# The second half of a v step: one piece per expert pair, or one piece per column half

## The chip, the cores and the metric

One Trainium2 chip, one core of it. The metric is the device time of one execution in microseconds, lower is better. The kernel before takes 3645.47 us, the median of three runs (3643.04 to 3650.47).

## What is computed

One encoder layer over 512 tokens of width 2048: two attention branches, gates, an output product, a layer norm, then PEER, a retrieval over 16384 experts, and a last layer norm. The change lies in PEER. Cut to it, the reference is:

```python
q = (h @ wq).reshape(bsz, s, PEER_HEADS, 2, PEER_HALF)
sc = jnp.einsum('bshpc,hpnc->bshpn', q, keys)
...                        # top 16 of each half, then top 16 of the sums: experts, and g by a softmax
def block(args):
    xt, et, gt = args
    a = jnp.einsum('td,thkd->thk', xt, u_tab[et])
    w = gt * jax.nn.gelu(a, approximate=False)
    return jnp.einsum('thk,thkd->td', w, v_tab[et])
```

Each token takes 128 expert rows of `u_tab` and of `v_tab`, 2048 wide, in float32.

## The kernel before

**Dense and gathered.** For 352 tokens the kernel does not gather: it goes through all 16384 experts with products on TensorE (u: scores of every expert; v: weighted sum), and the weight matrix is zero where an expert was not chosen. For the other 160 tokens it gathers rows of 1 MB (128 x 2048 float32) by an indirect DMA (L1083) and adds them up on VectorE (L1058 for u rows, L1064 for v rows). Both kinds of work run at the same time in the last 1500 us.

**Pieces.** Every matrix that TensorE needs comes as a stream of pieces of 128 x 1024 float32, 512 KB, in one fixed order (`seq`). Class `Stream` loads a piece on SP's queue (L80, tile `raw`), splits it into a high part `whi` on ScalarE (L99) and a residual `wlo` on VectorE (L100), since a product in float32 is made of three in a rounded form: high by high, high by low, low by high. `get` hands out the next piece and first calls `fill`, which sends out the splits of up to three pieces ahead and the loads of up to six. There are five buffers each for `raw`, `whi` and `wlo`. So the place of a `get` in the program sets where the split of a later piece stands in the queues of ScalarE and VectorE.

**Order.** `pin` keeps an instruction in program order on its engine. In the stage looked at here nearly all work of ScalarE, VectorE, POOL and TensorE is pinned.

**A round.** 128 experts make a chunk, four chunks (GE = 4) a group. For each group the kernel makes 4 u steps and, for the group before it, 4 v steps, one after the other: u step, v step, u step, v step. A u step (`u_mm`) takes two pieces, 24 products on each, and its Gelu (L1235) gives the scores of one chunk. Then `weigh` multiplies them with the gates (L1143 on VectorE) and splits the result into `W_h` (L1146, ScalarE) and `W_l` (L1147, VectorE). A v step (`v_mm`, index j) makes 512 columns of the output for all four chunks: four units of 128 columns (dd), each 12 products, 3 for each chunk x (L1181 to L1183). It takes two pieces, 24 products each in all. After each unit ScalarE evicts the bank (L1185) and puts the running sum of a later unit back into a bank (L1163), and an entry of `beside` is called: L1143 after unit 0, L1146 and L1147 after unit 1. After the last group of u, four v steps and then a stage of v steps alone follow, for 14 groups whose scores were made earlier and wait in memory; the last of these groups has its own form of the product (`v_part`).

**Gathered rows.** After each u step and each v step, `step` calls `gather` once or twice, by a rate of about 1.5. One call lets POOL copy one column of the youngest residual into the row's buffer (`paced`, L296), which holds the row back until that split is done, starts the row's DMA (L1083), and then lets VectorE use the row that was started two calls earlier. There are three row buffers.

**The v pieces before.** Piece x of step j of a group holds 512 columns for two chunks: chunk 0 and 1 in piece 0, chunk 2 and 3 in piece 1. Both are taken by `get` at the head of the step (L1169), and every unit uses both.

Of the kernel before, what the change touches and what calls it, by code (L numbers as in the profile page):

```python
# [19 lines left out]
P = 128  # L20
# [10 lines left out]
GE = 4  # L31
NG = 128 // GE
# [10 lines left out]
NF = sum(UQ) + UG * NCH  # L43
# [83 lines left out]
def tile_encoder_layer(ctx: ExitStack, tc: tile.TileContext, a: dict, out: bass.AP):  # L127
# [75 lines left out]
    def piece(k):  # L203
        if k[0] == "u":
            return a["u_t"][k[1], k[2]]
        if k[0] == "v":
            return a["v_t"][k[1], k[2], k[3]]
        return a["wst"][where[k]]
# [3 lines left out]
    def pin(op, level=1):  # L212


        if inorder[0] >= level:
            tc.keep_in_program_order(op)
        return op

    st = Stream(nc, wp, [(k, piece(k)) for k in seq], pin, 0, 0)
# [107 lines left out]
    with pool("p0", 3, "right") as p0:  # L327
# [70 lines left out]
        for i in range(8):  # L398
            g, t = i // 4, i % 4
# [14 lines left out]
        for g in range(2):  # L414
            vh, vl = [vp.tile([P, 4, 512], F32R, tag="v", name=f"va{g}{n}", bufs=4) for n in "hl"]
# [244 lines left out]
    with pool("attB", 2, "right") as wk:  # L660
# [7 lines left out]
        def v_b(grp):  # L668
            pss = [bank("sc") for _ in range(3)] + [bank("tp")]
            for k2 in range(2):  # L670
                wh, wl = st.get("vb", grp, k2)
                for kk in range(2):
                    k = k2 * 2 + kk
                    s = slice(kk * 512, kk * 512 + 512)
                    lh, ll = latn[4 + k]
                    for t in range(NT):
                        ts_ = slice(t * P, (t + 1) * P)
                        mm3(pss[t], (lh[:, ts_], ll[:, ts_]), (wh[:, s], wl[:, s]), k == 0, k == 3)
            return [split_to(wk, pss[t], f"v{t}", bufs=1) for t in range(NT)]

        prev = None
        v = None
        qr = {}
        for h in range(H + 1):
# [20 lines left out]
            if h < H and h % 4 == 0:  # L705
                v = v_b(h // 4)
# [449 lines left out]
    def o_bank():  # L1156
        nu[0] += 1
        return ob_[(nu[0] - 1) % 6]

    def copy_in(u):  # L1160

        if 16 <= u < nunits:
            pin(nc.scalar.activation(ob_[u % 6][:, :TD], accT[:, u % 16], AF.Copy), 2)  # L1163

    def v_mm(g, j, by=None, beside=()):

        v = [st.get("v", g, j, x) for x in range(2)]  # L1169
        beside = list(beside)  # L1170
        for dd in range(4):
            u = nu[0]
            o = o_bank()[:, :TD]
            sum_ = accT[:, j * 4 + dd]
            for x in range(GE):
                vh, vl = v[x // 2]
                wh, wl = W[g, x]
                s = slice(x % 2 * 512 + dd * P, x % 2 * 512 + (dd + 1) * P)
                first, last_ = u < 16 and x == 0, x == GE - 1
                kw = dict(skip_group_check=u >= 16)  # L1180
                pin(nc.tensor.matmul(o, vh[:, s], wh, start=first, stop=False, **kw), 2)  # L1181
                pin(nc.tensor.matmul(o, vh[:, s], wl, start=False, stop=False, **kw), 2)  # L1182
                pin(nc.tensor.matmul(o, vl[:, s], wh, start=False, stop=last_, **kw), 2)  # L1183
            if by is None:
                pin(nc.scalar.activation(sum_, o, AF.Copy), 2)  # L1185
            else:
                pin(nc.scalar.activation(sum_, o, AF.Copy, scale=by[:, j * 4 + dd : j * 4 + dd + 1]), 2)
            copy_in(u + 4)
            f = beside.pop(0) if beside else None
            if f is not None:  # L1190
                f()
        for f in beside:
            f()
# [27 lines left out]
    with pool("peer", 2, "right") as wk:  # L1221
# [8 lines left out]
        for n, g in enumerate(gorder):  # L1230
            gt = load_g(wk, g)
            for j in range(GE):
                gl = gl_of(g, j)
                ps = u_mm(g * GE + j)
                pin(nc.scalar.activation(gl, ps[:, :TD], AF.Gelu), 2)  # L1235
                if n > 0 or j > 1:
                    step()
                work = weigh(gl, gt, g, j)
                if n > 0:
                    v_mm(gorder[n - 1], j, None, work)  # L1240
                    step()
                else:
                    for f in work:
                        f()
# [11 lines left out]
    with pool("fin", 1, "right") as wk:  # L1256
# [36 lines left out]
        last = NF // GE - 1  # L1293
# [71 lines left out]
        for g in range(last + 1):  # L1365
# [19 lines left out]
            for j in range(GE):  # L1385
# [4 lines left out]
                elif j < 2:  # L1390
                    os_ = [start_sum(t, j) for t in range(ND)]
                    v = [st.get("v", g, j, x) for x in range(2)]
# [26 lines left out]
def _lay(inp):  # L1419

    f = lambda n: np.asarray(inp[n])
    w_in = f("w_in")[0]
    b_in = f("b_in")[0]
    o_q, o_k, o_v, o_c, o_kr, o_g = 0, 1024, 2048, 3072, 4096, 4160

    def fold(w):
        return w.reshape(-1, P, P).transpose(1, 0, 2).reshape(P, -1)

    def pairs(w, i):
        return w.reshape(-1, 2, P, 512)[i].transpose(1, 0, 2).reshape(P, 1024)  # L1430

    kr = w_in[:, o_kr : o_kr + 64]
    kr = np.concatenate([kr, kr], 1)
    uq = f("w_uq")[0].reshape(512, H, 192)
    ukv = f("w_ukv")[0].reshape(512, H, 256)
    pa, pb, wo, wq = f("w_pa")[0], f("w_pb")[0], f("w_o")[0], f("peer_wq")[0]

    def gcol(i):
        return o_g + (i % 2) * D + (i // 2) * P

    def piece(n, *k):
        hs = lambda w: fold(w[k[1] * 1024 : (k[1] + 1) * 1024])
        if n == "lat":
            return w_in[k[0] * P : (k[0] + 1) * P, o_c : o_c + 1024]
        if n == "va":
            return w_in[k[0] * P : (k[0] + 1) * P, o_v : o_v + 1024]
        if n == "kr":
            return fold(kr[k[0] * 1024 : (k[0] + 1) * 1024])
        if n in ("qa", "ka"):
            c = (o_q if n == "qa" else o_k) + k[0] * P  # L1450
            return hs(w_in[:, c : c + P])
        if n == "g":
            c = gcol(k[0])
            return hs(w_in[:, c : c + P])
        if n == "uqr":
            h = 4 * k[0]
            return fold(np.concatenate([uq[:, h + 2 * j : h + 2 * j + 2, 128:].reshape(512, P) for j in range(2)], 0))
        if n == "qk":
            return fold(np.concatenate([uq[:, k[0], :128], ukv[:, k[0], :128]], 0))
        if n == "vb":  # L1460
            return pairs(ukv[:, 4 * k[0] : 4 * k[0] + 4, 128:].reshape(512, 512), k[1])
        if n in ("pa", "pb"):
            return fold((pa if n == "pa" else pb)[:, k[0] * P : (k[0] + 1) * P])
        if n == "wo":
            return wo[k[0] * P : (k[0] + 1) * P, k[1] * 1024 : (k[1] + 1) * 1024]
        return hs(wq[:, k[0] * P : (k[0] + 1) * P])

    bt = [b_in[o_c + i * P : o_c + (i + 1) * P] for i in range(8)]
    bt.append(np.concatenate([b_in[o_kr : o_kr + 64]] * 2))
    bt += [b_in[i * P : (i + 1) * P] for i in range(16)]  # L1470
    bt += [b_in[gcol(i) : gcol(i) + P] for i in range(2 * KT)]
    x = f("x")[0]
    rel = np.clip(np.arange(P)[:, None] - np.arange(S)[None, :] + 384, -63, 256) + 63
    u = f("peer_u")[0]
    v = f("peer_v")[0]
    freq = (np.float32(10000.0) ** (-np.arange(0, 64, 2, dtype=np.float32) / np.float32(64.0))).astype(np.float32)
    rot = np.zeros((P, 2), np.float32)
    rot[:, 0] = np.tile(freq, 4)
    rot[:, 1] = np.tile(np.repeat(np.array([-1.0, 1.0], np.float32), 32), 2)
    return {  # L1480
        "x": x,
        "x_t": x.T.reshape(KT, P, S),
        "c_t": f("c").reshape(KT, P).T,
        "positions": f("positions").reshape(1, S),
        "w_ada_t": f("w_ada")[0].T.reshape(96, P, D),
        "b_ada_t": f("b_ada")[0].reshape(96, P).T,
        "wst": np.stack([piece(*k) for k in weight_keys()]),
        "b_in_t": np.stack(bt, 1),
        "b_va": b_in[o_v : o_v + 1024].reshape(1, 1024),
        "rms_g": np.concatenate([f("q_norm_g")[0].reshape(4, P), f("kv_norm_g")[0].reshape(4, P)]).T,  # L1490
        "rel_t": f("rel_bias")[0][:, rel],
        "rot_c": rot,
        "iota": np.tile(np.arange(P, dtype=np.float32), (P, 1)),
        "ln1_t": np.concatenate([f("ln1_g")[0].reshape(KT, P), f("ln1_b")[0].reshape(KT, P)]).T,
        "ln1_g": f("ln1_g"), "ln1_b": f("ln1_b"), "ln2_g": f("ln2_g"), "ln2_b": f("ln2_b"),
        "keys_t": f("peer_keys")[0].reshape(16, P, P).transpose(2, 0, 1).reshape(P, 16 * P),
        "u_t": u.reshape(P, P, 2, 8, P).transpose(1, 2, 4, 3, 0).reshape(P, 2, P, 1024),
        "v_t": v.reshape(P, NG, 2, 2, 4, 512).transpose(1, 4, 2, 0, 3, 5).reshape(NG, 4, 2, P, 1024),
        "peer_u": u,
        "peer_v": v,  # L1500
    }
# [17 lines left out]
```

## Time and profile before

| | us |
|---|---|
| median of 3 runs | 3645.47 |
| lowest, highest | 3643.04, 3650.47 |
| the profiled execution: its time | 3657.82 |
| its span, first to last instruction | 3656.0 |
| TensorE busy in it | 3568.4 (98%) |
| VectorE busy | 2695.8 (74%) |
| ScalarE busy | 1727.1 (47%) |
| GpSimd busy | 1002.2 (27%) |

A profile shows one execution. Times count from the first instruction. Engines: PE is TensorE's products, PEld its weight loads, DVE is VectorE, ACT ScalarE, POOL GpSimd, SP the queue that loads the pieces. In a row of the order in time, the first number is the start, the second how long it took; a bracket at the end gives how long the engine had been idle and what ended that; "x2" are two instructions of a kind in a row, merged. An engine's idle time counts only where TensorE, or the end, waits for it.

### The profile page before, as it was taken

Reading aid. Unit: us, or ns where it says so; the run is one execution under the profiler, and the core shown is the slowest. Engines: PE = TensorE matmul, PEld = TensorE weight load, DVE = VectorE, ACT = ScalarE, POOL = GpSimd, SP = SyncE. Lnnn points to the kernel's source line nnn. Section 1 sums busy time; section 2 is a strip of 40 time slices with the busy share of each in tenths; the row PEclk is TensorE's granted clock in tenths of the full one; section 3 lists DMA queues with packets and bytes.
Section 4 is the critical chain, followed back from the end, with each engine's and each line's share of the span. In section 5 each row is a group of like instructions: output and inputs, shape, how many; then the busy total and the mean of one; then the engine's idle time right before and its main releaser. Section 6 shows DMA issues by size and latency. Waiting matters only on the chain. (4 is left out here: it accounts for less than half of the span.)

```text
span 3656.0 us, 52881 instructions
## 1 busy us (share of the span) xinstructions
PE 3568.4 (98%) x20127; PEld 3285.5 (90%) x20127; DVE 2695.8 (74%) x3754; ACT 1727.1 (47%) x3072; POOL 1002.2 (27%) x1068
## 2 busy tenths in 40 slices
PE   8999999999999999999999999999999999899998
PEld 6888888887787889999999999999999999899997
DVE  8756587545555779988888678888777788677776
ACT  3233332233333455435666345555544455566763
POOL 0001110011120000002322344444454544455531
PEclk9999999999999999999999999999999999999999
DMA  9646488744356655446998899999989999799982
GB/s 395 259 164 227 165 303 301 261 141 130 115 193 241 203 197 159 130 132 234 339 349 329 313 355 357 351 365 360 355 327 343 331 362 368 298 345 341 346 326 93
DMA packets 216207, 996.71 MB, mean 273 GB/s; under 512 B 26817, under 2 KB 34161, under 8 KB 159345
## 3 DMA queue, kind: packets, MB, share of 16 engines
q1 hardware_dynamic: 131904, 525.93, 40.4%
q0 software_dynamic: 73104, 431.48, 31.5%
q10 hardware_dynamic: 10944, 35.94, 2.5%
q8 instruction: 157, 2.57, 0.3%
q14 instruction: 98, 0.79, 0.1%
HBM read 930.42 MB, written 61.51 MB: 271 GB/s over the span
## 5 line engine op out<-in xcount | busy, mean ns | idle before, releaser
L99 ACT ACTIVATE whi<-raw 128x1024 fp32r<-128x1024 f32 x800 | 822.7, 1055 | 773.8 <-PE main L160 491.9
L100 DVE TENSOR_TENSOR wlo<-raw,whi 128x1024 fp32r<-128x1024 f32 x800 | 959.4, 1221 | 284.1 <-ACT whi L99 280.0
L159 PE MATMUL q<-dh,whi 128*128 128x352 f32 x1680 | 546.2, 325 | 0.6 <-ACT glf L926 0.6
L161 PE MATMUL q<-dh,wlo 128*128 128x352 f32 x1680 | 542.1, 323 | 0.7 <-DVE wlo L100 0.7
L160 PE MATMUL q<-dl,whi 128*128 128x352 f32 x1680 | 542.5, 323 | 0.0
L296 POOL COPY row<-wlo 128x1 f32<-128x1 f32 x320 | 326.4, 1020 | 714.5 <-DVE wlo L100 519.7
L1064 DVE SCALAR_TENSOR_TENSOR h2g<-row,au,h2g 128x2048 f32<-128x2048 f32 x127 | 298.4, 2349 | 101.9 <-DMA row<-in_peer_v,gidx 99.3
L159 PE MATMUL main<-hh,whi 128*128 128x512 f32 x912 | 352.9, 394 | 10.1 <-ACT hh L354 9.9
L160 PE MATMUL main<-hl,whi 128*128 128x512 f32 x912 | 357.1, 392 | 0.0
L161 PE MATMUL main<-hh,wlo 128*128 128x512 f32 x912 | 349.4, 393 | 0.0
L1058 DVE SCALAR_TENSOR_TENSOR row<-row,h2g 128x2048 f32<-128x2048 f32 x128 | 292.6, 2288 | 76.8 <-DMA row<-in_peer_u,gidx 76.4
L161 PEld LDWEIGHTS q<-dh,wlo 128*128 128x128 f32 x1680 | 316.6, 188 | 1.0 <-DVE wlo L100 1.0
L159 PEld LDWEIGHTS q<-dh,whi 128*128 128x128 f32 x1680 | 316.5, 188 | 1.0 <-ACT glf L926 0.8
L160 PEld LDWEIGHTS q<-dl,whi 128*128 128x128 f32 x1680 | 317.0, 189 | 0.0
L1185 ACT ACTIVATE accT<-o 128x352 f32<-128x352 f32 x480 | 219.5, 458 | 184.2 <-PE o L1183 178.6
L300 DVE SCALAR_TENSOR_TENSOR adaw<-adaw,cond 128x2048 f32<-128x2048 f32 x96 | 218.8, 2291 | 100.7 <-DMA adaw<-in_w_ada_t 96.9
L159 PE MATMUL main<-qh,whi 128*128 128x352 f32 (+2 forms) x752 | 242.9, 323 | 7.5 <-ACT qs L950 7.4
L161 PE MATMUL main<-qh,wlo 128*128 128x352 f32 (+2 forms) x752 | 242.7, 323 | 0.0
L160 PE MATMUL main<-ql,whi 128*128 128x352 f32 (+2 forms) x752 | 242.0, 322 | 0.0
L1163 ACT ACTIVATE o<-accT 128x352 f32<-128x352 f32 x480 | 223.0, 465 | 0.0
L159 PEld LDWEIGHTS main<-hh,whi 128*128 128x128 f32 x912 | 172.1, 189 | 47.3 <-ACT hh L354 11.5
L161 PEld LDWEIGHTS main<-hh,wlo 128*128 128x128 f32 x912 | 171.7, 188 | 35.8
(1359 smaller groups left out, 8045.9 us busy)
## 6 DMA issues: line engine op xcount, KB each, us to landing
raw<-in_wst SPq DMA_DIRECT2D x288, 512.0 KB
raw<-in_u_t SPq DMA_DIRECT2D x256, 512.0 KB
raw<-in_v_t SPq DMA_DIRECT2D x256, 512.0 KB
adaw<-in_w_ada_t SPq DMA_DIRECT2D x96, 1024.0 KB
g_d<-stg ACTq DMA_DIRECT2D x11, 2048.0 KB
gt<-g_d POOLq DMA_DIRECT2D x19, 704.0 KB
ga_d<-glf ACTq DMA_DIRECT2D x56, 176.0 KB
gl<-ga_d POOLq DMA_DIRECT2D x56, 176.0 KB
```

Source lines behind the costliest of these rows:

```text
L99: self.pin(self.nc.scalar.activation(hi, raw, AF.Copy), 2)
L100: self.pin(self.nc.vector.tensor_tensor(out=lo, in0=raw, in1=hi.bitcast(F32), op=ALU.subtract))
L159: pin(nc.tensor.matmul(ps, lh, rh, start=first, stop=False), 2)
L160: pin(nc.tensor.matmul(ps, lh, rl, start=False, stop=False), 2)
L161: pin(nc.tensor.matmul(ps, ll, rh, start=False, stop=last), 2)
L296: return eng.tensor_copy(t[:, 0:1], src.bitcast(F32)[:, 0:1])
L300: pin(nc.vector.scalar_tensor_tensor(w, w, 1.0, cond, op0=ALU.mult, op1=ALU.mult, accum_out=mod[:, j : j + 1]))
L1058: op = nc.vector.scalar_tensor_tensor(row, row, 1.0, h_, op0=ALU.mult, op1=ALU.mult, accum_out=a_[:, c : c + 1])
L1064: op = nc.vector.scalar_tensor_tensor(accs[n], row, a_[:, c : c + 1], accs[n], op0=ALU.mult, op1=ALU.add)
L1163: pin(nc.scalar.activation(ob_[u % 6][:, :TD], accT[:, u % 16], AF.Copy), 2)
L1185: pin(nc.scalar.activation(sum_, o, AF.Copy), 2)
```

## The change

The v pieces are laid out anew on the host: the first piece of a step holds 256 columns of the width for all four chunks, the second the other 256 for all four. Units 0 and 1 use the first piece alone, units 2 and 3 the second alone, and each `get` stands ahead of the unit that begins with its piece, not both at the head. The last group keeps the old layout, since `v_part` takes its pieces in the old form. Numbers and sizes of transfers, splits and products are the same.

```diff
-        v = [st.get("v", g, j, x) for x in range(2)]
         beside = list(beside)
         for dd in range(4):
             u = nu[0]
             o = o_bank()[:, :TD]
             sum_ = accT[:, j * 4 + dd]
+            if dd % 2 == 0:
+                vh, vl = st.get("v", g, j, dd // 2)
             for x in range(GE):
-                vh, vl = v[x // 2]
                 wh, wl = W[g, x]
-                s = slice(x % 2 * 512 + dd * P, x % 2 * 512 + (dd + 1) * P)
+                s = slice(x * 256 + dd % 2 * P, x * 256 + (dd % 2 + 1) * P)
                 first, last_ = u < 16 and x == 0, x == GE - 1
...
+    vt = v.reshape(P, NG, GE, 4, 2, 256).transpose(1, 3, 4, 0, 2, 5).reshape(NG, 4, 2, P, 1024).copy()
+    last = NF // GE - 1
+    vt[last] = v.reshape(P, NG, 2, 2, 4, 512)[:, last].transpose(3, 1, 0, 2, 4).reshape(4, 2, P, 1024)
...
-        "v_t": v.reshape(P, NG, 2, 2, 4, 512).transpose(1, 4, 2, 0, 3, 5).reshape(NG, 4, 2, P, 1024),
+        "v_t": vt,
```

## Rows read from the trace of the kernel before

**Rows 1.** The page, part 1: busy us, share of the span, instructions.
```profile
PE 3568.4 (98%) x20127; PEld 3285.5 (90%) x20127; DVE 2695.8 (74%) x3754; ACT 1727.1 (47%) x3072; POOL 1002.2 (27%) x1068
```

**Rows 2.** The page, part 2: DMA engines' busy share, 40 slices of 91.4 us.
```profile
DMA  9646488744356655446998899999989999799982
```

**Rows 3.** Two stretches: us, PE, PEld, DVE, ACT, POOL busy (instructions), PEclk, DMA share, GB/s.
```profile
2400.00:2500.00 100.00, 100.00 (x631) 100.00 (x630) 82.11 (x81) 52.99 (x96) 46.67 (x43) 1.00 0.96 360
2700.00:2800.00 100.00, 93.67 (x572) 92.24 (x571) 75.76 (x56) 46.03 (x84) 52.13 (x38) 0.98 0.90 325
```

**Rows 4.** TensorE's waits, 2065 to 3109, then 3180 to 3560: us, times, longest.
```profile
PE o L1183 <- DVE wlo L100: 12.8, 9, 2.6
...
PE o L1183 <- DVE wlo L100: 3.4, 7, 0.9
```

**Rows 5.** TensorE in order of time: v steps' starts, a late second piece.
```profile
2065.80 0.32 PE L1181 MATMUL o<-W_0h,whi 128*128 128x352 f32 x1
...
3109.19 0.32 PE L1181 MATMUL o<-W_0h,whi 128*128 128x352 f32 x1
...
3125.56 0.32 PE L1182 MATMUL o<-W_2l,whi 128*128 128x352 f32 x1
3129.00 0.66 PE L1183 MATMUL o<-W_2h,wlo 128*128 128x352 f32 x1 [3.13 <-DVE wlo L100]
```

**Rows 6.** VectorE in order of time, one round from 2574.
```profile
2574.65 2.35 DVE L100 TENSOR_TENSOR wlo<-raw,whi 128x1024 fp32r<-128x1024 f32 x2
2576.93 0.52 DVE L1143 TENSOR_TENSOR gl<-gl,gt 128x352 f32<-128x352 f32 x1
2578.07 0.53 DVE L1147 TENSOR_TENSOR W_1l<-gl,W_1h 128x352 fp32r<-128x352 f32 x1 [0.62 <-ACT W_1h L1146]
2578.51 2.29 DVE L1058 SCALAR_TENSOR_TENSOR row<-row,h2gx 128x2048 f32<-128x2048 f32 x1
...
2582.03 2.36 DVE L100 TENSOR_TENSOR wlo<-raw,whi 128x1024 fp32r<-128x1024 f32 x2 [1.23 <-ACT whi L99]
...
2587.29 2.29 DVE L1058 SCALAR_TENSOR_TENSOR row<-row,h2gx 128x2048 f32<-128x2048 f32 x1 [0.28 <-DMA row<-in_peer_u,xidx]
...
2589.50 2.36 DVE L100 TENSOR_TENSOR wlo<-raw,whi 128x1024 fp32r<-128x1024 f32 x2
2591.78 0.52 DVE L1143 TENSOR_TENSOR gl<-gl,gt 128x352 f32<-128x352 f32 x1
```

**Rows 7.** ScalarE in the same round.
```profile
2572.57 0.47 ACT L1235 ACTIVATE gl<-q 128x352 f32<-128x352 f32 x1 [4.88 <-PE q L161]
...
2577.54 0.50 ACT L1146 ACTIVATE W_1h<-gl 128x352 fp32r<-128x352 f32 x1 [0.32 <-DVE gl L1143]
...
2580.95 2.00 ACT L99 ACTIVATE whi<-raw 128x1024 fp32r<-128x1024 f32 x2
```

**Rows 8.** POOL in the same round: copies and issues of gathered rows.
```profile
2572.31 0.96 POOL L1083 DMA_INDIRECT row<-in_peer_u,xidx  x1 [0.27 <-POOL row L296]
...
2577.08 0.41 POOL L296 COPY row<-wlo 128x1 f32<-128x1 f32 x1 [0.37 <-DVE wlo L100]
2577.79 0.96 POOL L1083 DMA_INDIRECT row<-in_peer_u,xidx  x1 [0.30 <-POOL row L296]
...
2592.64 0.96 POOL L1083 DMA_INDIRECT row<-in_peer_u,xidx  x1 [0.31 <-POOL row L296]
```

**Rows 9.** VectorE, then POOL, where a row follows the residuals at once.
```profile
2669.41 2.35 DVE L1064 SCALAR_TENSOR_TENSOR h2g<-row,au,h2g 128x2048 f32<-128x2048 f32 x1
...
2680.08 2.35 DVE L1064 SCALAR_TENSOR_TENSOR h2g<-row,au,h2g 128x2048 f32<-128x2048 f32 x1 [2.20 <-DMA row<-in_peer_v,gidx]
...
2695.45 2.35 DVE L1064 SCALAR_TENSOR_TENSOR h2g<-row,au,h2g 128x2048 f32<-128x2048 f32 x1 [2.38 <-DMA row<-in_peer_v,gidx]
...
2669.56 2.24 POOL L296 COPY row<-wlo 128x1 f32<-128x1 f32 x1 [6.85 <-DVE wlo L100]
2672.07 1.65 POOL L1083 DMA_INDIRECT row<-in_peer_v,gidx  x1 [0.27 <-POOL row L296]
...
2687.28 1.67 POOL L1083 DMA_INDIRECT row<-in_peer_v,gidx  x1 [0.27 <-POOL row L296]
```

## The prediction

> **What bounds the kernel now.** I read the engines' busy times first. TensorE is busy 98% of the span, no other engine over 74% [rows 1], and the change takes no product away; so it can only act through what TensorE waits for, or through a new wait. The slices then show where there is no room elsewhere: from about 1700 us on, the DMA engines stand at eight or nine tenths in nearly every slice [rows 2]. The table of stretches compares two pieces of the same stage. In 2400 to 2500 TensorE never idles and issues 631 products, so one takes 100/631 = 0.1585 us; in 2700 to 2800 it issues 572 and VectorE is less busy too [rows 3]. The list of TensorE's waits names the cause: in the stage of alternating u and v pieces the only wait is of a product in L1183 for the residual that VectorE makes in L100, 12.8 us in 9 waits; in the v-only stage the same wait has 3.4 us [rows 4]. Which product it is shows in TensorE's order in time: the two products of expert 2 with the high part run, and the third, `W_2h` by `wlo`, waits [rows 5]. Expert 2 is the first one of the second piece. So the second piece of a step comes late by up to 3.1 us, while the first is there.
>
> A **round** of the u/v stage is one u step and one v step, 96 products: 96 x 0.1585 = 15.2 us for TensorE alone. From the v step that starts at 2065.80 to the one at 3109.19 [rows 5] there are 67 rounds (17 groups of 4, less one), 15.57 us each.
>
> **What is removed: the early need of the second piece.** The third product on the second piece is the 9th of a v step now and the 27th then, so its residual may come 18 x 0.1585 = 2.85 us later. Every wait but one is shorter than that [rows 4, 5]. If nothing else moved, nearly all of the 12.8 + 3.4 us would go. Products, bytes, weight loads, evictions and copies stay the same in number and size; the layout is made on the host, and each piece still is one transfer of 512 KB with whole lines. Cost of all that: nothing.
>
> **What is moved: the second `get`.** It stood ahead of the products and stands behind two of the four units. Each `get` sends out one split (L99 on ScalarE, L100 on VectorE), and these engines keep program order. In a v step the splits now run as a pair: VectorE's two residuals from 2574.65, then the weighting (L1143 at 2576.93, L1147 at 2578.07), then a gathered row (L1058 at 2578.51) [rows 6]. After the change the order is residual, L1143, L1147, residual, gathered row: the weighting hangs on units 0 and 1, the second `get` comes behind them. The second L99 also falls behind L1146 on ScalarE, which waits for L1143. The raw loads on SP follow the residuals and are spaced out likewise; in the round shown neither L99 nor L100 waits for a raw load [rows 6, 7], so I cost that at nothing (if that cover went, a late load would show as a wait of L99).
>
> **Who waits behind it: the gathered rows.** POOL starts each 1 MB row only after a small copy from the youngest residual (L296, then L1083). In a v step that is the residual that moves. Now the copy falls into VectorE's gap before L1147 and takes 0.41 us: 2577.08, row issued 2577.79 [rows 8]. After the change VectorE goes from the residual straight to a gathered row, and such a case is in the trace: the residuals end, L1064 starts at 2669.41, the copy needs 2.24 us (till that row is used up), and the issue is at 2672.07, 2.66 us after L1064 began [rows 9]. This row is used by VectorE in the next u step, just ahead of the residual that starts the next round's chain. So it closes a **loop** of one turn per round. Now: row used 2587.29, next row of this kind issued 2592.64 [rows 6, 8], 5.35 us, plus the row's own time from issue to use, 9.50 us (2577.79 to 2587.29, a wait of 0.28 among it): 14.85, just under TensorE's 15.2. After: use of the row to the next operation 2.21 (2587.29 to 2589.50); one residual 1.14 (half of 2589.50 to 2591.78); L1143 to L1146 0.61 (2576.93 to 2577.54); L1146 0.50; L99 to its residual 1.08 (2580.95 to 2582.03) [rows 6, 7]; residual 1.14; row start to issue 2.66 [rows 9]. Sum 9.34 us, so a turn costs 9.3 plus the row's time from issue to use.
>
> That time is the unknown. In the 9.50 the row stands behind the row issued at 2575; coming some 4 us later it will not, so 9.5 is too much. Bound above: rows that were issued with none in front and that VectorE then waited for, 2672.07 to 2680.08 and 2687.28 to 2695.45, 8.0 and 8.2 us [rows 9]; the same two raw loads start beside them as would here, but two had been started just before, against one here. Bound below: a row issued at 2572.31 and used without a wait at 2578.51, at most 6.2 us [rows 6, 8], with a short issue (0.96) and no raw load started beside it. Our case lies between, so I take the middle of 6.2 and 8.0, 7.1, and keep both ends. A round then is 9.3 + 7.1 = **16.4 us**, more than TensorE's 15.2: the loop becomes the bound.
>
> The Trainium skill ("DMA: Bandwidth & Descriptors", Anatomy of one DMA) gives a transfer from this queue 2.0 us and its bytes at 436 GB/s, an estimate of 4.4 us for 1 MB. By that a turn would be 13.7 us, TensorE would stay the bound, and the change would only gain; the rows that VectorE waited for took 8.0 and 8.2 us from issue to use with the DMA engines at 90% and more [rows 3, 9], so this trace does not agree.
>
> **The sum.** VectorE may fall back before TensorE feels it: the residual ready at about 2575.8 (the first of 2574.65) is for the second half of the next u step, 48 + 24 products after the v step began; that begins about where the Gelu does, 2572.57 [rows 7], so the need is at 2572.6 + 11.4 = 2584, and the slack about 8 us. 67 x 16.4 - 8 = 1091 us against 1043.4 now: +47. In the v-only stage POOL starts a row behind L1147 and not behind the residual, and VectorE's order before L1143 keeps both residuals ahead of it, so no such loop arises there; the 3.4 us go: -3. The stretch between the stages and the end I leave as they are: there the second piece is late by 3.13 us [rows 5], but the chain runs through loads of `gl`; -3 to +8 goes into the range. Together **+44 us** on the profiled execution's own 3657.8 (span 3656.0), 3702. The median of the runs is 12.3 lower, so 3645.5 + 44 = **3690**.
>
> **The rivals.**
> 1. *Faster: the row's time falls below 6.2 once it is issued later*, since fewer transfers stand in front. The mechanism is the removed wait alone; the point from which it decides is a row time of 15.2 - 9.3 = 5.9. At 6.2: 67 x 15.5 - 8 - 1043.4 = -13, and -3: 3629; at 5.9 and below the stage runs at TensorE's pace, 67 x 15.2 = 1018: -25 and -3: 3618. For it: TensorE runs without a stall in 2400 to 2500 [rows 3] while rows take 9.5 us, so part of that is queueing. Against: the two rows issued with none in front and waited for took 8.0 and 8.2 [rows 9]. I put it at 3626. That the page's rule above would decide is part of this case.
> 2. *No change*: at a row time of about 6.5 a turn is 15.8, 67 x 15.8 - 8 = 1051, +7 and -3; what the second piece gains the loop takes. 3649.
> 3. *Much slower: the row takes the full 8.0* of [rows 9]: 67 x 17.3 - 8 - 1043.4 = +108, -3: 3750. For it: the raw loads beside it are the same; against: one fewer in front, and a slower round also thins the other traffic.
> 4. *The change does not do what it says*: the second `get` could send out its split early because the order of pinned work is not kept. Every VectorE row of the stage stands in program order, so this has next to no weight and is counted with case 2.
>
> **How the numbers follow.** Forecast (row time 6.6 to 7.6, 3655 to 3720) 45%, rival 3 25%, rival 2 10%, rival 1 20%. What a measurement of this kernel can tell from no change is about 0.2%, 7 us. So slower 0.70, same 0.10, faster 0.20. The range reaches from 3625, inside rival 1, to 3750, inside rival 3; what it leaves out is the lower half of rival 1 and the upper part of rival 3.
>
> **What would show it.** In the u/v stage of the changed kernel: one L100 at a time in a v step, the second of them behind L1147; L296 there at 2 us and more, not 0.41; a round of about 16.4 us; VectorE waiting for the row ahead of the first residual in nearly every round; and TensorE's wait no longer at `W_2h`, but at the second piece of a u step (L161 for `wlo`), whose slack is smallest, with the first piece of a v step close by. DMA share and GB/s of the stage fall. It is wrong if the rounds stay at 15.2 to 15.3 us, if the copy still slips through a gap, or if the row's time falls to 6 us; and wrong in size by 67 us for each microsecond of the row's time.

## The result, and the profile after

| | before | after |
|---|---|---|
| median, us | 3647.97 (3643.04 to 3654.65) | 3802.31 (3797.2 to 3811.31) |
| ratio | | 1.0413, interval 1.0385 to 1.0442 |
| profiled execution: time, span, us | 3657.82, 3656.0 | 3811.31, 3809.5 |
| u/v stage, 67 rounds, us | 1043.4 | 1192.4 |
| one round, us | 15.57 | 17.80 |

The forecast was 3690 with a range of 3625 to 3750: the sign was right, and the time is 52 us above the range. Of the 153.5 us by which the profiled span grew, 149.0 lie in the u/v stage.

The page after, parts 1 and 2 (busy us, share of the span; DMA engines' busy share in 40 slices), and part 4, the chain of work that ended last. They answer to [rows 1, 2]:

```profile
PE 3616.8 (95%) x20127; PEld 3309.9 (87%) x20127; DVE 2701.9 (71%) x3754; ACT 1721.6 (45%) x3072; POOL 1085.9 (29%) x1068
...
DMA  9655588553466654449988887888887788889983
...
PE 49%; issue 18%; DMA 13%; POOL 12%; DVE 6%; ACT 2%; POOLq 0%; DVEq 0%; SPq 0%; ACTq 0%
```

TensorE is down to 95%, and the DMA slices fell from 9 and 8 to 8 and 7: more time for the same bytes. The chain runs through DMA and POOL for a quarter of the span, most of it gathered rows, their copies and their issues; POOL is busy for 29%, so a view of busy time would not have named it.

The two stretches of [rows 3], and the v steps at the two ends of the stage, for [rows 5]:

```profile
2400.00:2500.00 100.00, 93.16 (x569) 92.00 (x570) 72.24 (x71) 46.14 (x84) 49.62 (x38) 0.98 0.84 310
2700.00:2800.00 100.00, 88.83 (x520) 86.10 (x519) 66.17 (x50) 41.11 (x76) 49.22 (x37) 0.95 0.79 294
```

```profile
2066.39 0.32 PE L1181 MATMUL o<-W_0h,whi 128*128 128x352 f32 x1
...
2572.88 0.43 PE L161 MATMUL q<-dh,wlo 128*128 128x352 f32 x1 [1.45 <-DVE wlo L100]
...
3258.80 0.32 PE L1181 MATMUL o<-W_0h,whi 128*128 128x352 f32 x1
```

From 2066.39 to 3258.80 is the stage. The stretch that had 631 products has 569. TensorE's waits in the stage, and then those in the stage of v steps alone (3330 to 3705), for [rows 4]:

```profile
PE q L161 <- DVE wlo L100: 50.3, 29, 6.4
PE o L1183 <- DVE wlo L100: 42.2, 40, 2.4
PE o L1181 <- ACT whi L99: 17.0, 7, 3.8
...
PE o L1181 <- ACT W_3h L1146: 7.5, 5, 2.5
PE o L1181 <- ACT o L1163: 2.3, 1, 2.3
```

The worst wait moved to the second piece of a u step (L161). L1183 still waits, no longer at `W_2h` but, in 31 of the 40 cases, at the first product of unit 2, where the second piece now begins.

One round of VectorE, then POOL, where [rows 6, 8] stood:

```profile
2569.39 2.29 DVE L1058 SCALAR_TENSOR_TENSOR row<-row,h2gx 128x2048 f32<-128x2048 f32 x1 [3.62 <-DMA row<-in_peer_u,xidx]
...
2571.61 1.22 DVE L100 TENSOR_TENSOR wlo<-raw,whi 128x1024 fp32r<-128x1024 f32 x1
2572.76 0.53 DVE L1143 TENSOR_TENSOR gl<-gl,gt 128x352 f32<-128x352 f32 x1
2573.91 0.53 DVE L1147 TENSOR_TENSOR W_0l<-gl,W_0h 128x352 fp32r<-128x352 f32 x1 [0.63 <-ACT W_0h L1146]
2574.86 1.23 DVE L100 TENSOR_TENSOR wlo<-raw,whi 128x1024 fp32r<-128x1024 f32 x1 [0.42 <-ACT whi L99]
2576.00 2.28 DVE L1058 SCALAR_TENSOR_TENSOR row<-row,h2gx 128x2048 f32<-128x2048 f32 x1
...
2586.53 2.29 DVE L1058 SCALAR_TENSOR_TENSOR row<-row,h2gx 128x2048 f32<-128x2048 f32 x1 [3.75 <-DMA row<-in_peer_u,xidx]
```

```profile
2576.15 2.18 POOL L296 COPY row<-wlo 128x1 f32<-128x1 f32 x1 [7.66 <-DVE wlo L100]
2578.60 1.66 POOL L1083 DMA_INDIRECT row<-in_peer_u,xidx  x1 [0.27 <-POOL row L296]
```

This is the forecast loop: row used at 2569.39, residual, L1143, L1147, the second residual behind them, the next gathered row at once, the copy 2.18 us behind it, the issue at 2578.60, the row used at 2586.53. Use to issue is 9.21 us (median of the stage 9.3; forecast 9.34). The row's time is 7.93 here, 7.69 in the median (forecast 7.1, rival 3: 8.0). The median turn, use to use, is 17.04 us.

A median turn of 17.04 and a mean round of 17.80 do not agree: 19 of the 67 rounds take over 18.5 us, so something comes on top in some rounds. VectorE's waits for loads in the stage show it, and one case in order of time, on VectorE and on POOL:

```profile
DVE h2g L1064 <- DMA row<-in_peer_v,gidx: 101.9, 36, 6.0
DVE row L1058 <- DMA row<-in_peer_u,gidx: 83.5, 30, 4.1
DVE gl L1143 <- DMA gt<-g_d: 57.0, 11, 7.7
```

```profile
2148.84 0.53 DVE L1143 TENSOR_TENSOR gl<-gl,gt 128x352 f32<-128x352 f32 x1 [6.06 <-DMA gt<-g_d]
...
2131.34 2.18 POOL L296 COPY row<-wlo 128x1 f32<-128x1 f32 x1 [7.75 <-DVE wlo L100]
...
2138.57 1.12 POOL L1134 DMA_DIRECT2D gt<-g_d  x1
```

At the head of a group the gates' load (`load_g`, L1134, 704 KB) stands on POOL's queue behind rows that wait for their residual. In ten of the 17 groups of the stage it is issued only 4.2 to 8.8 us before VectorE is ready for it, and used 9.3 to 12.3 us after its issue. In the kernel before it was issued 9.1 to 15.0 us ahead of its use, and VectorE waited 3.2 us for it in the whole stage, in three times. The forecast has no term for it.

### The profile page after: what moved, and what is told of

Its sections match the earlier page's. It is cut to its first block, busy times and chain, and to the rows that moved or that the text cites. A ratio compares the mean times of both kernels' runs of the same rounds, so it can differ in the third digit from the quotient of the medians.

```text
span 3809.5 us, 52874 instructions
## 1 busy us (share of the span) xinstructions
PE 3616.8 (95%) x20127; PEld 3309.9 (87%) x20127; DVE 2701.9 (71%) x3754; ACT 1721.6 (45%) x3072; POOL 1085.9 (29%) x1068
## 4 chain that ended last, share of the span: by engine, by line
PE 49%; issue 18%; DMA 13%; POOL 12%; DVE 6%; ACT 2%; POOLq 0%; DVEq 0%; SPq 0%; ACTq 0%
PE main L161 11%; PE main L159 11%; PE main L160 11%; POOL row L296 6%; DMA row<-in_peer_v,gidx 6%; POOL row L1083 5%; DVE wlo L100 3%; DMA adaw<-in_w_ada_t 3%; PE o L1182 2%; PE o L1183 2%; PE o L1181 2%; DMA gt<-g_d 1%; PE q L159 1%; PE q L161 1%; PE q L160 1%
## 5 line engine op out<-in xcount | busy, mean ns | idle before, releaser
L99 ACT ACTIVATE whi<-raw 128x1024 fp32r<-128x1024 f32 x800 | 835.5, 1056 | 770.0 <-PE main L160 474.1
L161 PE MATMUL q<-dh,wlo 128*128 128x352 f32 x1680 | 553.8, 330 | 51.5 <-DVE wlo L100 51.0
L296 POOL COPY row<-wlo 128x1 f32<-128x1 f32 x320 | 365.0, 1141 | 815.6 <-DVE wlo L100 695.0
L161 PEld LDWEIGHTS q<-dh,wlo 128*128 128x128 f32 x1680 | 320.9, 191 | 65.9 <-DVE wlo L100 65.1
L161 PE MATMUL main<-hh,wlo 128*128 128x512 f32 x912 | 348.9, 392 | 0.2 <-DVE wlo L100 0.2
L161 PE MATMUL main<-qh,wlo 128*128 128x352 f32 (+2 forms) x752 | 242.6, 323 | 0.0
L1163 ACT ACTIVATE o<-accT 128x352 f32<-128x352 f32 x480 | 223.6, 466 | 0.0
L1083 POOL DMA_INDIRECT row<-in_peer_v,gidx x128 | 197.8, 1545 | 37.8 <-POOL row L296 32.3
```

Source lines behind the costliest of these rows:

```text
L99: self.pin(self.nc.scalar.activation(hi, raw, AF.Copy), 2)
L161: pin(nc.tensor.matmul(ps, ll, rh, start=False, stop=last), 2)
L296: return eng.tensor_copy(t[:, 0:1], src.bitcast(F32)[:, 0:1])
L1083: pin(nc.gpsimd.indirect_dma_start(out=row, out_offset=None, in_=src, in_offset=off), 2)
```

## The experiments

All are compared with the kernel before on the same chip. That kernel read 3648 us beside the kernel after, 3668 beside a1 to a4, 3652 beside b1 to b4, 3673 beside c2 to e2 and 3671 beside f1 and f2; so ratios are compared, and the length of the u/v stage in each profile. A stage is that of one profiled execution: b4, equal to the kernel before by its ratio, shows 8.8 us less.

| kernel | ratio to before (interval) | stage, us | round, us |
|---|---|---|---|
| before | 1 | 1043.4 | 15.57 |
| after | 1.0413 (1.0385 to 1.0442) | 1192.4 | 17.80 |
| a1: layout only | 0.9979 (0.9962 to 0.9997) | 1041.2 | 15.54 |
| a2: split moved only | 1.0302 (1.0278 to 1.0325) | 1154.5 | 17.23 |
| a3: after, older residual in v steps | 0.9941 (0.9923 to 0.9959) | 1041.5 | 15.54 |
| a4: after, gates earlier | 1.0177 (1.0149 to 1.0204) | 1093.9 | 16.33 |
| b1: after, weighting behind the split | 0.9973 (0.996 to 0.9986) | 1030.9 | 15.39 |
| b2: a3 and a4 | 0.9972 (0.9956 to 0.9988) | 1026.4 | 15.32 |
| b3: b1 and a4 | 0.9971 (0.9959 to 0.9983) | 1036.0 | 15.46 |
| b4: before, gates earlier | 1.0003 (0.9991 to 1.0015) | 1034.6 | 15.44 |
| c2: after, row held longer | 1.059 (1.0551 to 1.0629) | 1258.7 | 18.79 |
| c3: before, row held longer | 1.0038 (1.0016 to 1.0061) | 1064.0 | 15.88 |
| e1: a1, older residual in u steps | 0.9919 (0.9895 to 0.9942) | 1022.4 | 15.26 |
| e2: a3, older residual in u steps too | 0.9907 (0.9884 to 0.9929) | 1022.4 | 15.26 |
| f1: before, older residual in u steps | 0.9913 (0.9899 to 0.9927) | 1022.4 | 15.26 |
| f2: after, gates on SP's queue | 1.0263 (1.0242 to 1.0285) | 1143.0 | 17.06 |

### Which half of the change costs: a1 and a2

a1 has the new layout with both `get`s at the head of the step; a2 has the old layout with the second split moved.

```diff
# a1, against after
+        v = [st.get("v", g, j, x) for x in range(2)]
...
-            if dd % 2 == 0:
-                vh, vl = st.get("v", g, j, dd // 2)
+            vh, vl = v[dd // 2]
# a2, against before
-        v = [st.get("v", g, j, x) for x in range(2)]
+        v = [st.get("v", g, j, x, fill=x == 0) for x in range(2)]
...
+            if dd == 2:
+                st.fill()
```

> The new layout (256 columns for all four chunks) with both gets left at the head of the v step, so no split moves. Loop theory (the loss comes from the moved split, which holds back a gathered row and closes a turn of 9.3 us plus the row's time): the loop stays as in the kernel before, the second piece is needed 18 products later, so the waits of L1183 for L100 (12.8 us in the alternating stage) go: 3618 to 3635 us, faster than the kernel before. Rival, the layout itself costs (loads of the new pieces, or products that use them): about 3800 us, like the changed kernel. Rival, the late second piece only shows a lack elsewhere and the wait turns up at another product: 3640 to 3650.

> The old layout and both gets at the head, but the split that the second get sends out stands behind unit 1, where the changed kernel has it. Loop theory: rounds of 17 us as in the changed kernel, 3790 to 3830 us, with TensorE's waits at the second piece of the v step (needed 18 products earlier than in the new layout) and of the u step. Rival, the layout is what costs: 3640 to 3660 us.

a1 gained 0.2% (its interval ends at 0.03% and 0.4%), a2 lost 3.0%. In a2 the turn is 16.93 us in the median, the use to issue 9.3, the row 7.6: the loop comes with the moved split alone, also in the old layout. But a2's loss is smaller than was expected (its ratio times 3648 gives 3758 us, not 3790 to 3830), and its stage is 38 us shorter than that of the kernel after. Its waits for the gates are 36.0 us and not 57.0, and 20 of its held-back rows (7 in the kernel after) are issued in 0.96 us and then take 5.7; what the layout has to do with either no run shows. And a1 did not do what the forecast said of a later need. L1183's waits in its stage:

```profile
PE o L1183 <- DVE wlo L100: 13.7, 10, 2.7
```

13.7 us, where the kernel before has 12.8 [rows 4]. They moved to the first product of unit 2, 18 products further, and did not shrink.

### What closes the loop: a3, b1, c2 and c3

In a3 the copy that releases a row in a v step reads the residual made before the youngest (`older` is 1 during that `step`). In b1 the weighting runs behind units 2 and 3, so the split is not behind it.

```diff
# a3, against after
-        src = st.parts[max(st.parts)][1] if src is None else src
+        src = st.parts[max(st.parts) - older[0]][1] if src is None else src
...
                     v_mm(gorder[n - 1], j, None, work)
+                    older[0] = 1
                     step()
+                    older[0] = 0
# b1, against after
-                    v_mm(gorder[n - 1], j, None, work)
+                    v_mm(gorder[n - 1], j, None, [None, None] + work)
```

> The changed kernel, but in a v step POOL's copy that holds a gathered row back reads the residual before the youngest, so that the row does not wait for the moved split; all splits stay where the change put them. Loop theory: from the row's use to the next issue 2.2 + 1.1 + 0.9 = about 4.2 us in place of 9.3, a turn of at most 14 us, TensorE is the bound again, and the gates' load (behind the rows on POOL) is early too: 3615 to 3655 us. Rival, the moved split hurts by itself, by ScalarE's evictions that now stand behind L1146 and L99: about 3800 us.

> The changed kernel, but L1143 stands behind unit 2 and L1146, L1147 behind unit 3 of the v step, so behind the second split and not ahead of it; the youngest residual still holds the row back. Loop theory: from a row's use to the next issue 5.35 us again (two residuals, L1143, the copy in the gap ahead of L1147), not 9.3; the turn falls under TensorE's 15.2: 3640 to 3665 us, within 0.5% of the kernel before. Rival, that splits one by one in the middle of the v step are what costs: 3720 us or more.

Both came out as the loop theory expected: either edit alone takes the 149 us away and more. In a3 the splits stay where the change put them, VectorE still waits for `whi` 30.4 us in 68 times, as in the kernel after (29.5 in 69), and that costs nothing. So neither the late split nor ScalarE's order hurt; what hurts is a row held back until that split. In b1 the copy falls into VectorE's gap ahead of L1147 again:

```profile
2577.75 0.41 POOL L296 COPY row<-wlo 128x1 f32<-128x1 f32 x1 [0.37 <-DVE wlo L100]
2578.47 0.96 POOL L1083 DMA_INDIRECT row<-in_peer_u,xidx  x1 [0.30 <-POOL row L296]
```

c2 and c3 lengthen one link: in v steps POOL clears half of the row's buffer between copy and issue (the row then overwrites it).

```diff
# c2 against after, c3 against before: in gather; hold is set during the step of a v step
                 pin(paced(row, None, nc.gpsimd), 2)
+                if hold[0]:
+                    pin(nc.gpsimd.memset(row[:, :1024], 0.0), 2)
```

> The kernel after, and in v steps POOL also clears half of the row's buffer between the copy (L296) and the row's DMA, so the row that closes the loop starts later by the time H of that clear. Theory (the loop of use, residual, weighting, residual, gathered row, copy, issue, row's time sets the round): nothing hides H, the round grows from 17.0 by H, so the stage grows by 67 us per microsecond of H: with H of 1 us some 3870 us against 3802, with H of 2 us some 3935. Rival (the round is set by the amount of traffic, and the row's issue is only one of many things that come late): H is hidden, 3800 to 3815.

> The kernel before with the same clear between copy and DMA of the row in v steps. Its turn was worked out at 5.35 + 9.50 = 14.85 us beside TensorE's 15.2, and part of the 9.50 is standing behind another row. Theory: the loop is not the bound here and part of H is taken from the queueing, so H of 1 us costs little, at most 67 x (14.85 + 1 - 15.57) = 19 us, 3650 to 3670, and with H of 2 us at most some 85 us. Rival (the clear itself costs time wherever it stands, for instance by holding up VectorE): the same rise as in the kernel after, some 65 us per microsecond of H.

Copy, clear and issue in c2:

```profile
2566.06 2.18 POOL L296 COPY row<-wlo 128x1 f32<-128x1 f32 x1 [10.36 <-DVE wlo L100]
2568.30 0.96 POOL L1083 MEMSET row<- 128x1024 f32 x1
2569.53 1.79 POOL L1087 DMA_INDIRECT row<-in_peer_u,xidx  x1 [0.27 <-POOL row L1083]
```

(The edit moves lines: L1083 is the clear here, L1087 the issue.) From the copy's start to the issue are 3.47 us here and 2.45 in the kernel after: 1.02 us more. The mean round grew by 18.79 - 17.80 = 0.99, and the stage by 66 us; the ratio times 3648 gives 3863 us, near the 3870 expected.

But that 1.02 and 0.99 agree is luck. Rounds 1 to 18 and 37 to 54 grew by 4.4 and by -5.4 us in all: there the issue took 2.73 and 2.96 us in the kernel after (medians), beside a gathered-row operation of VectorE, and takes 1.73 and 1.96 here, so the clear stands in time that the issue lost before. Rounds 19 to 36 and 55 to 67 grew by 42.7 and 24.6 us, 2.2 a round: there the issue takes no less, and the row's time from the issue's end to the use rose from 6.2 to 7.6 us, for which no run gives a reason. So c2 shows that a later issue lengthens the round, and not that each turn grows by the link.

In the kernel before the same clear costs 0.4%; the stage grew by 1064.0 - 1043.4 = 20.6 us, 0.31 a round, just over the 19 that were worked out as its bound. There the use to issue grew from 5.37 to 6.34 us (medians), and the row's time fell from 9.67 to 8.78.

### The term without a price: a4, b2, b3, b4, f2

In a4 the gates of the next group are loaded at j = 2 of the group before, on the same queue.

```diff
# a4, against after; b4 is the same against before; b2 and b3 add it to a3 and b1
+        gt_next = load_g(wk, gorder[0])
...
-            gt = load_g(wk, g)
+            gt = gt_next
...
+                if j == 2:
+                    gt_next = load_g(wk, gorder[n + 1] if n + 1 < len(gorder) else 0)
# f2, against after, in load_g
-        pin(nc.gpsimd.dma_start(gt, g_d[:, :, g * GE : (g + 1) * GE, :]), 2)
+        pin(nc.sync.dma_start(gt, g_d[:, :, g * GE : (g + 1) * GE, :]), 2)
```

> The changed kernel with the load of the next group's gates (gt, 704 KB on POOL's queue) sent out in the third u step of the group before, not at the group's head. VectorE's L1143 waits 57 us for it in 11 waits in the changed kernel. If these waits lie on the loop: 3745 to 3770 us, rounds of 17.0 us without the long ones. If the time is hidden anyway, since the row behind it comes as late: 3790 to 3805 us.

> The changed kernel with both cures, the older residual for the copy in a v step and the gates' load in the third u step of the group before. In the kernel with the first cure alone L1143 still waits 32 us for the gates in 17 waits, and TensorE's waits in the stage are 12 us. If the gates' waits delay the residuals there too: another 5 to 10 us off, 0.990 to 0.993 of the kernel before. If they are hidden now that the loop has slack: 0.994 again.

> The weighting behind both splits, as in the run before it, and the gates' load early. Loop theory: as that run, less what L1143 still waits for the gates: 3630 to 3660 us. Rival, none of the gates' wait matters once the weighting stands last: no difference between the two.

> The kernel before, with the gates' load early alone. It waits 3.2 us in 3 waits for the gates, so early loading is worth nothing here if the gain in the changed kernel came from its own late waits: 3640 to 3670 us, ratio 0.998 to 1.002. If early loading is worth something by itself, since it spreads the transfers: 0.990 to 0.997, and then the changed kernel's gain from it was no sign of a wait on its loop.

> The kernel after, with the gates' load (gt, 704 KB for each group) on SP's queue and not on POOL's, at the same place in the program. Theory (on POOL it stands behind the copies that hold back the rows): VectorE's wait for gt at L1143 falls from 57 us to under 15, and the stage comes near the 1094 us of the run that loads it earlier; 3725 to 3740. Rival (its bytes come at a bad moment, whatever the queue): the wait stays at 40 us or more and the time near 3800.

VectorE's wait for `gt` is gone in a4 and in f2. f2 leaves the load at the same place in the program, with the same bytes, on another queue. Its stage is 1143.0, 49.4 us less than after; so its place on POOL's queue costs that. The queue also sets the moment: f2 issues the load 20.4 to 30.1 us ahead of its use, a4 36 to 44, the kernel after 9.3 to 12.3. No run moves the load to another queue at the same moment, so that its bytes come at a bad moment is not excluded. Nor is 49.4 a fixed price: a2, with the old layout and the load on POOL's queue, waits 36.0 us for it, and its stage is only 11.5 us longer than f2's. What is left in f2 is the loop and little else: 67 rounds of 17.06, with a turn of 16.98 in the median, use to issue 9.26 and the row 7.71. TensorE's waits in f2:

```profile
PE q L161 <- DVE wlo L100: 50.3, 35, 6.7
PE o L1183 <- DVE wlo L100: 31.9, 31, 1.4
```

f2's 1143 is not the 1094 that was expected, and a4 came out faster than its 3745 to 3770 (its ratio times 3648 gives 3713). In a4, 28 of the 67 rounds take under 15.6 us, in f2 11. The use to issue is 9.2 to 9.3 us in the median in both. What differs is behind it: in 33 rounds of a4 (4 of f2) the held-back row's issue takes 0.96 us, in nearly all others 1.65 to 3.0; in a4 the former rows are used 6.5 us after their issue in the median, the others 7.7; and in 20 rounds (1 in f2) VectorE does not wait for the row. Why a4 has more of them was not settled. In the kernel before, early gates are worth nothing (b4), and beside a cure of the loop they add nothing that the ratios show (b3 against b1; b2, at 0.9972, is not below a3, at 0.9941, where 0.990 to 0.994 was expected). The term comes with the held-back rows, not with the gates alone.

### What the kernel before really waited for: e1, e2, f1

a1's waits that did not shrink asked for another cause. It stands in [rows 9] already, where the rows are those issued in u steps: 2672.07 issued, 2680.08 used, 2687.28 issued, 2695.45 used. Use to use is 15.37 us, more than the 15.26 of a round in which TensorE does not wait. That is a second loop, through the row of a u step. The edits cut it: during the `step` of a u step the copy reads a residual two splits older.

```diff
# e1 against a1, e2 against a3, f1 against before (each with the line in paced, as in a3)
                 if n > 0 or j > 1:
+                    older[0] = 2
                     step()
+                    older[0] = 0
```

> The new layout with both gets at the head (as in the run with the layout alone), and in u steps the copy that releases a row reads a residual two splits older, so that the row of a u step starts sooner. Theory (the 13.7 us of waits at L1183 that stayed with the layout alone come from the row issued in a u step, in rounds with one row in the u step and two in the v step, a second loop slower than TensorE): these waits fall to under 4 us, ratio to the kernel before 0.990 to 0.996. Rival (the waits come from the splits' own place, or from the DMA traffic): 10 us of waits or more stay, ratio 0.998.

> The kernel after with the older residual for the copy in v steps (as in the run that brought the round back to 15.54) and a residual two splits older in u steps too: both loops are cut. Theory: the second loop was what kept the 11.4 us of waits at the third product of a unit; they go, the stage comes near 67 x 15.2 to 15.3 = 1018 to 1025 us, ratio 0.989 to 0.994, the fastest version. Rival (the gates' load behind held-back rows, 32 us of VectorE's waits in that run, is what remains): ratio 0.994 as there.

> The kernel before, old layout and both gets at the head, with one edit: in u steps the copy that releases a row reads a residual two splits older. Theory (the splits of the kernel before come late by the loop over the row of a u step; the early need of the second piece only shows where a split is late already): the waits at L1183 go (under 2 us), the stage takes 1022 to 1026 us as with the new layout and the same edit, ratio 0.991 to 0.995. Rival (the early need costs something by itself): 5 us of waits or more stay at the third product of expert 2, the stage takes 1030 us or more, ratio 0.996 or more.

All three come to a stage of 1022.4 us. The whole stage of f1 and of the kernel after in one row each (us, then busy us and instructions of PE, PEld, DVE, ACT, POOL, then TensorE's clock, DMA share, GB/s):

```profile
2071.00:3094.00 1023.00, 1023.00 (x6438) 1023.00 (x6437) 837.54 (x718) 525.13 (x930) 426.83 (x421) 1.00 0.94 359
```

```profile
2066.00:3259.00 1193.00, 1080.92 (x6438) 1052.27 (x6437) 834.92 (x716) 510.83 (x930) 568.17 (x421) 0.97 0.82 307
```

In f1 TensorE is busy in 1023.00 of 1023.00 us, with the old layout, in which every unit needs both pieces. So the early need of the second piece cost nothing in itself; it was only where a split that was late already showed first. e1 (new layout) and f1 (old) have overlapping intervals: with this loop cut the layout is worth nothing that shows, and without the cut a1's 0.2% is all. e2, with the change and both loops cut, has the lowest ratio, 0.9907, and its interval overlaps theirs too.

## Why the prediction was right in sign and wrong in size

**Right: the loop.** Each link came as worked out: single residuals, the second behind L1147, the copy at 2.18 us (2.24 from [rows 9]), use to issue 9.3 for 9.34, VectorE waiting for the row ahead of the residual, DMA share from 0.94 down to 0.82. a2 shows it without the layout, a3 and b1 remove it, and c2, which issues the row later, lengthens the stage by 66 us.

**Mis-sized: the row's time, 7.1 for 7.7.** The step that failed is "I take the middle of 6.2 and 8.0". The bounds were right and the choice between them was not. The low end came from a row whose issue took 0.96 us, the high end from rows issued behind a gathered-row operation, in 1.65 us, and waited for, which is the state that the loop itself makes. In the kernel after 60 of the 67 held-back rows have an issue of 1.64 us or more, and these rows take 7.7 us in the median; the seven with 0.96 take 5.7. The median of all is 7.69. Worth 67 x 0.6 = 40 us. f2, which has the loop without the other term, measures the forecast's sum by itself: 1143.0 against 1091 forecast, 99.6 us over the kernel before and not 47. Of the remaining 12 us: the first seven rounds of f2 ran at 15.2 to 15.3 us, which is the slack of the forecast, but six others took 19.2 to 25.9, which no step of it foresaw; their cause stays open.

**Missing: the gates' load.** The change does not touch it, and of what waits on POOL's queue behind the moved split the forecast priced the rows alone. `load_g` stands on the same queue: once rows on it are held longer, it is late too, at the head of ten of the 17 groups, and VectorE's L1143 waits for it inside the loop. 49.4 us by f2. It was readable before: the trace lists that wait with 3.2 us in three times, so in three groups it had no slack to lose. 99.6 + 49.4 make the 149.0.

**Wrong: "if nothing else moved, nearly all of the 12.8 + 3.4 us would go".** a1 is that case and kept 13.7 us in the u/v stage; in the v-only stage of the kernel after the L1183 wait did go, but waits of L1181, 7.5 us for `W_3h` and 2.3 us for L1163, remained (5.5 us of the former in the kernel before). The diagnosis stopped at the product that waits; it had to go on to why the residual was late. VectorE's lag ran through the row of a u step, whose turn of 15.37 was in the rows quoted, while the forecast worked out the turn of a v step's row alone (14.85). So rival 1's prices of 3618 to 3629 rested on a gain that was not there for the taking.

**The place of the waits** was half right: the second piece of a u step leads with 50.3 us, but the next is the second piece of a v step, not the first.

**Rival 3** (row time 8.0, 3750) named the nearer row time, and without the gates its sum, 67 x 17.3 - 8 = 1151, is close to f2's 1143.

The Trainium skill's figure for such a transfer ("DMA: Bandwidth & Descriptors", Anatomy of one DMA), from which an estimate of 4.4 us for 1 MB was worked out, would have left TensorE the bound; the rows took 7.7 us from issue to use in the median, with the DMA engines 82% busy, so it does not hold as a price in this kernel.

## What to carry to other kernels

When a step is moved behind other work, ask what is released by it and write out the whole turn, from one use of the buffer to the next use: if it exceeds the bound engine's period, it costs its excess in every round. Then walk each in-order queue the released work stands on and price every other thing queued there, even what the diff does not touch. Before crediting the removal of a wait, ask why its releaser was late: moving the need by 18 products bought 0.2%, while releasing a copy from an older tile bought 0.9%.

## What the runs showed of the hardware

A 128x1 copy on POOL takes 0.18 to 0.41 us where VectorE leaves a gap or runs a short operation, and mostly 2.18 or 2.24 where it starts behind a gathered-row operation (up to 4.9 in the kernel before). c2's clear of 128x1024 does not depend on that. Copy and clear in one step of c2, each beside a gathered-row operation:

```profile
2098.46 2.29 DVE L1058 SCALAR_TENSOR_TENSOR row<-row,h2g 128x2048 f32<-128x2048 f32 x1
2098.61 2.18 POOL L296 COPY row<-wlo 128x1 f32<-128x1 f32 x1 [7.38 <-DVE wlo L100]
...
2100.67 2.29 DVE L1058 SCALAR_TENSOR_TENSOR row<-row,h2g 128x2048 f32<-128x2048 f32 x1
2100.85 0.96 POOL L1083 MEMSET row<- 128x1024 f32 x1
```

All 105 clears of c2 took 0.95 to 1.01 us, 95 of them wholly inside one VectorE operation; in c3, where 4 were, they took 0.95 or 0.96. So it is not VectorE's being busy as such that holds POOL up. The Trainium skill ("SBUF — State Buffer", SBUF: two separate sides) says that a VectorE operation with two inputs in SBUF blocks a GpSimd operation only if that one reads SBUF; the trace agrees: the copy reads, the clear does not. The issue of a gathered row (L1083) is held up as well: in the stage of the kernel after it took 0.96 to 0.98 us in the 88 cases with VectorE idle for its first 0.96 us, 1.65 to 1.69 in the 68 beside residuals, and up to 3.08 beside a gathered-row operation.

TensorE's clock can fall when it stands still. In the kernel after, one wait of 5.15 us and the products behind it, then the granted clock (third column from the end) over the next stretches:

```profile
2401.15 0.66 PE L161 MATMUL q<-dh,wlo 128*128 128x352 f32 x1 [5.15 <-DVE wlo L100]
2401.61 0.50 PE L159 MATMUL q<-dh,whi 128*128 128x352 f32 x1
2401.90 0.50 PE L160 MATMUL q<-dl,whi 128*128 128x352 f32 x1
```

```profile
2401.00:2403.00 2.00, 1.85 (x6) 1.85 (x7) 1.06 (x3) 1.38 (x3) 0.00 (x0) 0.54 0.66 197
2403.00:2406.00 3.00, 3.00 (x15) 3.00 (x15) 2.89 (x2) 3.00 (x7) 1.60 (x1) 0.74 0.41 131
2406.00:2412.00 6.00, 6.00 (x40) 6.00 (x39) 5.02 (x6) 3.50 (x7) 5.09 (x4) 1.00 0.75 259
```

After the wait the granted clock is 0.54, about the lower of its two levels (1.2 of 2.4 GHz), and products come 0.29 us apart instead of 0.16 until it is back at 1.00. Over the stage TensorE was busy 1080.92 us where f1 needed 1023.00 for as many products. So of the 170 us between the two stages 58 appear as busy time and 112 as waits. The granted clock of 0.97 accounts for about half of the 58 (0.03 of 1081 is 32, an estimate); the rest stays open.
